# An up projection of the second layer's FFN as seven block products, with token halves of 320

## The chip, the cores and the metric

The kernel runs as one program on one NeuronCore of a Trainium2 chip. Its metric is the device time of one execution in microseconds, and the time given is the median of three executions. The engines are TensorE (PE, with its weight loads as a row of their own, PEld), VectorE (DVE), ScalarE (ACT), GpSimd (POOL) and SyncE (SP, which here only issues DMAs).

## The reference, cut to what matters

The reference is two layers of a transformer step over 640 tokens (128 prompt tokens and 512 latent tokens) of width 1024. A layer runs three token mixers, gates and an output projection; then comes the FFN, where the change lies.

```python
D_MODEL, D_FF = 1024, 2816
def _swiglu(h, w_in, w_out):
    a, b = jnp.split(h @ w_in, 2, axis=-1)      # w_in: 1024 x 5632
    return (jax.nn.silu(a) * b) @ w_out          # w_out: 2816 x 1024
def _layer(x, mod, lw, ...):
    sh1, sc1, g1, sh2, sc2, g2 = jnp.split(mod, 6, axis=-1)
    ...
    h = _rmsnorm(x, lw['norm2_g']) * (1.0 + sc2) + sh2
    x = x + g2 * _swiglu(h, lw['w_ffn_in'], lw['w_ffn_out'])
```

All inputs and outputs are float32.

## The kernel before

**Layout.** Activations lie transposed: 128 channels on the partitions, `KT` = 8 channel tiles, tokens along the free axis. The 640 tokens are cut in two halves, `HALF`: half 0 holds 256 tokens (128 prompt, 128 latent) and half 1 holds 384. Every operand of a large product is held as two float32r tiles, `hi` (a rounded copy, made on ACT by `split_hi`) and `lo` (the rest, made on DVE by `split_lo`, which subtracts `hi` from the value). Each product is three matmuls that accumulate in one PSUM bank: hi x hi, hi x lo, lo x hi (`mm3` and `mm_outer`).

**Weights.** `load_w` fetches a block of 128 x up to 1024 floats with one DMA on the SP queue into one of three `raw` buffers, and splits it into one of four `whi` and one of four `wlo` buffers. The buffers therefore set how far ahead weights can be fetched and split.

**FFN.** D_FF is cut in `FT` = 22 column tiles f of 128 columns. For each f and each half, `up_mm` computes a and b (2 outputs x 8 channel tiles x 3 matmuls = 48 matmuls), and `up_end` makes silu(a) * b (ACT, then DVE) and splits it into `ghi` and `glo`. The f are worked in parts, `FFN_PARTS` = 8, 8 and 6; after each part, `down` multiplies the part's g by the down weights for each of 8 output tiles n and both halves, and `x_add` adds the result to x. The first two f stand apart: their half 0 runs first, their half 1 behind it, so that `norm2(1)` (the normalisation of half 1) can run meanwhile. At the end of the last part and of the output projection, `tail` runs the last four n of one half first and then those of the other; before the last three units it calls `mid`, which starts the next normalisation on DVE and ACT.

**Order.** The program is written in one order, and a list scheduler places each instruction on its engine's queue when its operands and buffers are ready by its own reckoning, earliest in the program first; the queues then run in order. `plan` and `fill` deal out background work (in the first layer's FFN, the modulation rows `ada_rows` on DVE) at counted points.

Of the kernel before, what the change touches and what calls it, by code (L numbers as in the profile page):

```python
# [28 lines left out]
HALF = ((0, 256), (256, 384))  # L29
# [7 lines left out]
FFN_PARTS = ((0, 8), (8, 16), (16, 22))  # L37
# [10 lines left out]
class Kern:  # L48
    def __init__(self, ctx, nc, tc, io):
# [6 lines left out]
        self.hp = self.sb("hp", 1)  # L56
        self.w = self.sb("w", 4)
# [196 lines left out]
    def groups(self, h):  # L254
        return ((0, 0, 128), (1, 128, 256)) if h == 0 else ((1, 0, 384),)

    def square(self, h, k, x, pool):

        n = HALF[h][1]
        if k == 0:  # L260
            ss = self.ss[h] = pool.tile([P, 384], F32, tag="nss", name="nss", bufs=2)
            self.act.activation(ss[:, :n], x[:, k, :], AF.Square)
        else:
            ss = self.ss[h]
            sq = pool.tile([P, 384], F32, tag="nsq", name="nsq", bufs=2)
            self.act.activation(sq[:, :n], x[:, k, :], AF.Square)
            self.dve.tensor_tensor(ss[:, :n], ss[:, :n], sq[:, :n], op=ALU.add)
# [4 lines left out]
    def rstd(self, h, pool, ps, summed=False):  # L272
# [3 lines left out]
        r = pool.tile([P, 384], F32, tag="nr", name="nr", bufs=2)  # L276
# [4 lines left out]
    def h_tiles(self, h):  # L281
        n = HALF[h][1]
        return [self.hp.tile([P, KT, n], F32R, tag=f"h{h}{p}", name=f"h{h}{p}") for p in ("hi", "lo")]

    def modulate(self, l, which, h, k, xn, a, ht, pool):
# [4 lines left out]
        u = pool.tile([P, 384], F32, tag="nu", name="nu", bufs=2)  # L290
# [9 lines left out]
    def norm(self, l, which, h, x, a, pool, ps):  # L300
# [4 lines left out]
        for k in range(KT):  # L305
            t = pool.tile([P, 384], F32, tag="nt", name="nt", bufs=2)
            self.dve.tensor_tensor(t[:, :n], x[:, k, :], r[:, :n], op=ALU.mult)
            self.modulate(l, which, h, k, t[:, :n], a, ht, pool)
        return ht

    def start(self):
# [30 lines left out]
        for h in (0, 1):  # L342
            n = HALF[h][1]
            ps = self.Tp()
            for k in range(KT):
                sq = xp.tile([P, 384], F32, tag="nsq", name="nsq", bufs=2)
# [448 lines left out]
    def ret_values(self, l, act, pool):  # L795

        self.rproj = [self.dr.tile([P, NB, 256], F32, tag=f"rp{j}", name="rproj", bufs=1) for j in range(4)]
        for j in range(4):
            units = self.load_a(self.io["w_ret"][l, 2 + j], 2, 4, 256)
            for b in range(NB):  # L800
                ps = self.G()
                self.a_gemm(ps[:, :256], act, b, units)
                r = pool.tile([P, 384], F32, tag="gt", name="rvs", bufs=2)
# [200 lines left out]
    def gates(self, l, g, act, m, pool):  # L1004

        for n in range(KT):
            u = self.load_w(self.io["w_gate"][l, g, n], 1024)
            for h in (0, 1):
# [3 lines left out]
                t = pool.tile([P, 384], F32, tag="gt", name="gt", bufs=2)  # L1012
# [4 lines left out]
    def branch(self, l, g, act, yhi, ylo, m, pool, last):  # L1017
# [5 lines left out]
        def unit(n, h):  # L1023
# [4 lines left out]
            t = pool.tile([P, 384], F32, tag="gt", name="gt", bufs=2)  # L1028
# [26 lines left out]
    def m_split(self, m, h):  # L1055
        n = HALF[h][1]
        hi = self.hp.tile([P, KT, n], F32R, tag=f"h{h}hi", name=f"m{h}hi")
        lo = self.hp.tile([P, KT, n], F32R, tag=f"h{h}lo", name=f"m{h}lo")
# [20 lines left out]
    def out_proj(self, l, act, x, pool, mid):  # L1079
        wu = {}  # L1080

        def unit(n, h):
# [4 lines left out]
            self.square(h, n, x[h], pool)  # L1087
# [23 lines left out]
    def ffn(self, l, act, x, pool, xp, hook, a, b, mid):  # L1111
# [3 lines left out]

        def up_mm(fs, h, outs, hook=None):
            w = HALF[h][1]
            self.mm_outer([o[:, :w] for o in outs], [self.b_steps(*wu[f, j], 0, KT, act, h) for f in fs for j in range(2)], hook)

        def up_end(f, h, pa, pb):  # L1120
            o, w = HALF[h]
            s = pool.tile([P, 384], F32, tag="fs", name="fs", bufs=2)
            self.act.activation(s[:, :w], pa[:, :w], AF.Silu)
            self.dve.tensor_tensor(s[:, :w], s[:, :w], pb[:, :w], op=ALU.mult)
            self.split_hi(g[f][0][:, o:o + w], s[:, :w])
            self.split_lo(g[f][1][:, o:o + w], s[:, :w], g[f][0][:, o:o + w])
# [18 lines left out]
        for pi, (f0, f1) in enumerate(FFN_PARTS):  # L1145
            lastp = pi == len(FFN_PARTS) - 1
            for f in range(max(f0, 2), f1):
                load(f)
# [7 lines left out]
            if lastp:  # L1156
                self.log_exp_table()

            def down(n, h):
# [6 lines left out]
                if lastp:  # L1166
                    self.square(h, n, x[h], xp)
# [25 lines left out]
    def run(self):  # L1193
# [3 lines left out]
        for l in range(DEPTH):  # L1197
            if l > 0:
                xsrc = []
                for h in (0, 1):  # L1200
                    dt = self.dr.tile([P, KT, HALF[h][1]], F32, name=f"xs{h}")
                    self.pool.dma_start(out=dt, in_=x[h])
                    xsrc.append(dt)
                xctx.close()
# [31 lines left out]
            x = self.load_x(xp, xsrc)  # L1236
            mact = {}
# [13 lines left out]
            act2, nxt = {}, {}  # L1251

            def norm2(h, ps):
# [8 lines left out]
                act2[h] = self.norm(l, 1, h, x[h], norm2.a, xp, ps)  # L1262
            self.out_proj(l, mact, x, xp, lambda: norm2(0, self.Tp()))
            with ExitStack() as c3:
                fp = self.sb("ffn", 1, c3)
                if l == 0:
                    self.plan(34, (chain(self.ada_rows(0, 40, 48, adp), self.ada_rows(1, 0, 48, adp)), 56))

                    def norm1(h):
                        if h == 0:  # L1270
                            norm1.a = self.mod_scale(1, 0)
                        nxt[h] = self.norm(1, 0, h, x[h], norm1.a, xp, self.Tp())
                    self.ffn(l, act2, x, fp, xp, lambda ps: norm2(1, ps), 0, 1, lambda: norm1(0))
                else:
                    self.plan(34)
                    rf = []
# [136 lines left out]
```

## Time and profile before

| | |
|---|---|
| median of 3 executions (us) | 2488.35 (2484.45 to 2488.82) |
| time of the profiled execution (us) | 2487.65 |
| span of its profile, first to last instruction (us) | 2485.8 |
| mean granted TensorE clock | 0.996 |
| busy: PE, DVE, ACT, POOL (us) | 2419.1, 1511.3, 992.8, 177.0 |

The profile is of one execution. Busy time counts the instructions of an engine; matmuls are pipelined, so that their durations overlap and the distance from one start to the next is what a matmul costs. A line number is one of the code above, and can be that of a helper (L112 is `split_hi`, L115 `split_lo`, L120 the weight DMA).

### The profile page before, as it was taken

To read this page: it belongs to the slowest core of one execution; us is meant where nothing else is said; L and a number is where in the kernel's file an instruction comes from. 1 tells how busy PE (TensorE), PEld (TensorE's weight loads), DVE (VectorE), ACT (ScalarE), POOL (GpSimd) and SP (SyncE) were. 2 spreads that over 40 slices of the span, in tenths; PEclk is the share of its full clock that TensorE was granted. 3 is DMA by queue.
4 is the path that set the end of the run, shared out by engine and by line. 5 is a ranking of instruction groups with operands and counts; after the bars stand their busy time and mean duration, and the time that the engine had idled before them with its cause. 6 is when DMAs were issued, how large, how long until landed. Compare 5 with 4: busy or idle time off the path is not lost.

```text
span 2485.8 us, 42801 instructions
## 1 busy us (share of the span) xinstructions
PE 2419.1 (97%) x17236; PEld 2367.1 (95%) x17236; DVE 1511.3 (61%) x3463; ACT 992.8 (40%) x2102; POOL 177.0 (7%) x306
## 2 busy tenths in 40 slices
PE   8999999999999999999999999998999999999998
PEld 5999999999999999999999999998999999999997
DVE  5877686566787676485477867764663553333324
ACT  5656565422335221212375655653222352122123
POOL 0000210100010010010000012111000000000001
PEclk9999999999999999999999999999999999999999
DMA  6212322322553454463231123213232222222221
GB/s 263 75 60 63 105 78 65 96 91 70 196 175 111 153 178 153 128 193 102 66 126 55 60 75 114 69 61 126 62 109 69 77 68 85 78 69 76 69 75 62
DMA packets 70677, 248.94 MB, mean 100 GB/s; under 512 B 9840, under 2 KB 10064, under 8 KB 69584
## 3 DMA queue, kind: packets, MB, share of 16 engines
q1 hardware_dynamic: 46944, 164.12, 20.3%
q0 software_dynamic: 23248, 81.36, 10.1%
q8 instruction: 135, 2.21, 0.4%
q10 hardware_dynamic: 288, 0.73, 0.1%
q14 instruction: 62, 0.51, 0.1%
HBM read 225.97 MB, written 20.22 MB: 99 GB/s over the span
## 4 chain that ended last, share of the span: by engine, by line
PE 91%; DVE 4%; issue 2%; ACT 2%; DMA 1%; POOL 0%; DVEq 0%; ACTq 0%; POOLq 0%
PE G L131 13%; PE G L132 12%; PE G L133 12%; PE S L1107 8%; PE S L1106 8%; PE S L1105 8%; PE S L131 6%; PE S L132 6%; PE S L133 6%; PE O L855 1%; PE Tp L658 1%; PE S L825 1%; PE O L633 1%; PE O L632 1%; PE S L826 1%
## 5 line engine op out<-in xcount | busy, mean ns | idle before, releaser
L112 ACT CAST whi<-raw 128x1024 fp32r<-128x1024 f32 (+4 forms) x298 | 299.2, 1018 | 756.5 <-PE G L132 262.5
L115 DVE TENSOR_TENSOR wlo<-raw,whi 128x1024 fp32r<-128x1024 f32 (+4 forms) x298 | 349.2, 1182 | 370.7 <-ACT whi L112 368.6
L131 PE MATMUL G<-ghi,whi 128*128 128x256 f32 (+1 forms) x704 | 217.1, 309 | 3.1 <-DVE x L1067 3.1
L133 PE MATMUL G<-ghi,wlo 128*128 128x384 f32 (+1 forms) x704 | 216.4, 308 | 0.0
L132 PE MATMUL G<-glo,whi 128*128 128x384 f32 (+1 forms) x704 | 216.3, 308 | 0.0
L1105 PE MATMUL S<-h1hi,whi 128*128 128x384 f32 x640 | 214.0, 334 | 0.0
L1106 PE MATMUL S<-h1lo,whi 128*128 128x384 f32 x640 | 213.9, 334 | 0.0
L1107 PE MATMUL S<-h1hi,wlo 128*128 128x384 f32 x640 | 213.9, 334 | 0.0
L1107 PE MATMUL S<-h0hi,wlo 128*128 128x256 f32 x704 | 199.2, 283 | 1.1 <-DVE wlo L115 0.9
L1106 PE MATMUL S<-h0lo,whi 128*128 128x256 f32 x704 | 198.8, 283 | 0.0
L1105 PE MATMUL S<-h0hi,whi 128*128 128x256 f32 x704 | 198.1, 282 | 0.0
L238 DVE SCALAR_TENSOR_TENSOR junk<-rawr,csr 128x1024 bf16<-128x1024 f32 x160 | 195.0, 1219 | 1.3
L131 PE MATMUL G<-whi,h1hi 128*128 128x256 f32 x624 | 179.0, 287 | 1.5 <-DVE mx L449 0.6
L133 PE MATMUL G<-whi,h1lo 128*128 128x256 f32 x624 | 177.2, 284 | 0.0
L132 PE MATMUL G<-wlo,h1hi 128*128 128x256 f32 x624 | 177.2, 284 | 0.0
L1067 DVE SCALAR_TENSOR_TENSOR x<-G,mod,x 128x128 f32<-128x128 f32 (+1 forms) x192 | 77.4, 435 | 138.0 <-PE G L133 137.5
L448 DVE TENSOR_REDUCE mx<-S 128x1 f32<-128x640 f32 (+1 forms) x160 | 113.0, 714 | 49.4 <-PE S L826 28.5
L1107 PEld LDWEIGHTS S<-h0hi,wlo 128*128 128x128 f32 x704 | 134.6, 191 | 2.8 <-DVE wlo L115 2.6
L131 PEld LDWEIGHTS G<-ghi,whi 128*128 128x128 f32 x704 | 132.1, 188 | 4.6 <-DVE x L1067 3.4
L1106 PEld LDWEIGHTS S<-h0lo,whi 128*128 128x128 f32 x704 | 134.3, 191 | 0.3
L1105 PEld LDWEIGHTS S<-h0hi,whi 128*128 128x128 f32 x704 | 134.3, 191 | 0.0
L131 PE MATMUL G<-whi,h0hi 128*128 128x256 f32 x416 | 121.6, 293 | 12.0 <-DVE rvs L808 11.7
(431 smaller groups left out, 6901.8 us busy)
## 6 DMA issues: line engine op xcount, KB each, us to landing
raw<-w_ffn_in SPq DMA_DIRECT2D x88, 512.0 KB, 3.6
rawr<-w_adat POOLq DMA_DIRECT2D x80, 512.0 KB, 4.0
raw<-w_gate SPq DMA_DIRECT2D x48, 512.0 KB, 3.3
raw<-w_ffn_out SPq DMA_DIRECT2D x32, 512.0 KB, 3.7
raw<-w_diff SPq DMA_DIRECT2D x24, 512.0 KB, 3.5
raw<-w_branch SPq DMA_DIRECT2D x24, 512.0 KB, 3.6
raw<-w_ret SPq DMA_DIRECT2D x24, 512.0 KB, 3.5
raw<-w_ada SPq DMA_DIRECT2D x16, 512.0 KB, 9.7
```

The costliest lines, as they stand in the source:

```text
L112: (eng or self.act).copy(hi, src)
L115: (eng or self.dve).tensor_tensor(lo, src, hi.bitcast(F32), op=ALU.subtract)
L131: self.pe.matmul(out, lh, rh, start=i == 0, stop=False)
L132: self.pe.matmul(out, lh, rl, start=False, stop=False)
L133: self.pe.matmul(out, ll, rh, start=False, stop=i == n - 1)
L238: self.tc.keep_in_program_order(d.scalar_tensor_tensor(junk, raw, 1.0, self.csr[:, i, :], op0=ALU.mult, op1=ALU.mult, accum_out=mod[:, n, ...
L448: self.dve.tensor_reduce(mx, sv, axis=AX.XY if len(sv.shape) == 3 else AX.X, op=ALU.max)
L632: self.pe.matmul(o[:, :n], vv, hi, start=i == 0, stop=False)
L1067: self.dve.scalar_tensor_tensor(x[h][:, n, c0:c1], ps[:, c0:c1], g[:, n, gi:gi + 1], x[h][:, n, c0:c1], op0=ALU.mult, op1=ALU.add)
L1105: self.pe.matmul(o, lh, rh, start=k == 0, stop=False)
L1106: self.pe.matmul(o, lh, rl, start=False, stop=False)
L1107: self.pe.matmul(o, ll, rh, start=False, stop=k == nk - 1)
```

## The change

The second layer's FFN computes f = 2 to 21 by Strassen's scheme. The product is seen as a 2 x 2 block product: the weights by (a, b) and by upper and lower half of the 1024 channels, the activations by channel half and token half. Seven block products of 128 x 512 by 512 x 320 take the place of eight. For that:

- `HALF` becomes 320 and 320 in the whole kernel. The hi and lo of the activations become one pair of tiles of 640 tokens, `self.ht`. Output tensors y0, y1 and the inputs x0, x1 follow.
- `w_ffn_in` is stored on the host as blocks (a upper, b lower) and (b upper, a lower). The first layer, and f = 0 and 1 of the second, still run eight products, from these blocks (`up_steps`).
- `ffn_forms`, once: `norm` of the second layer leaves its float32 result in eight tiles `us`; from them DVE makes the sums and differences of activation blocks, and ACT and DVE split them. One of them replaces the upper channels of half 1 in `ht`.
- `ffn_weights`, for each f: two loads as before (`r`, `q`), a third load of `r`'s block into `t` (two buffers), and an accumulating DMA on the POOL queue that adds the first block of the second source, twice, to both halves of `t`. DVE makes two further sums in `q`. Splits: 1024 columns of `r`, 512 of `q`, 1024 of `t`, 1024 of the new `q`.
- `ffn_seven`, for each f: seven products of 12 matmuls of 320 columns, and the combination of the results on DVE and ACT in the tiles `v` and `u` (one buffer each).
- `FFN_PARTS` becomes 6, 6, 5 and 5 in both layers, and `ghi`, `glo` have 6 buffers instead of 10. The scratch of the norms moves into a pool of its own, which is closed before `ffn_forms` and opened again for the last part. `plan` of the first layer's FFN follows the new number of points.

```diff
-HALF = ((0, 256), (256, 384))
+HW = 320
+HALF = ((0, HW), (HW, HW))
...
-FFN_PARTS = ((0, 8), (8, 16), (16, 22))
+FFN_PARTS = ((0, 6), (6, 12), (12, 17), (17, 22))
+GB = 6
+NC = 2
...
+        self.ht = [self.hp.tile([P, KT, T], F32R, name=f"h{p}") for p in ("hi", "lo")]
...
-        return ((0, 0, 128), (1, 128, 256)) if h == 0 else ((1, 0, 384),)
+        return ((0, 0, 128), (1, 128, HW)) if h == 0 else ((1, 0, HW),)
...
+    def modulate(self, l, which, h, k, xn, a, ht, pool, u=None):
 
         n = HALF[h][1]
         sh = self.mod[l][:, 24 * which:24 * which + 8, :]
         hi, lo = ht
-        u = pool.tile([P, 384], F32, tag="nu", name="nu", bufs=2)
+        if u is None:
+            u = pool.tile([P, HW], F32, tag="nu", name="nu", bufs=2)
...
+        hi, lo = self.ht
+        return hi[:, k, 128 * b:128 * b + 128], lo[:, k, 128 * b:128 * b + 128]
...
+    def ffn_forms(self, pool, us):
+        d = self.dve
+        hh, hl = self.ht
+        fo, so = slice(0, HW), slice(HW, T)
+        x67 = [pool.tile([P, 4, T], F32R, name=f"x67{p}") for p in ("hi", "lo")]
+        x5 = [pool.tile([P, 4, HW], F32R, name=f"x5{p}") for p in ("hi", "lo")]
+        for k in range(4):
+            p, q = us[k], us[4 + k]
+            d.tensor_tensor(q[:, so], q[:, so], p[:, so], op=ALU.subtract)
+            d.tensor_tensor(p[:, so], p[:, fo], p[:, so], op=ALU.subtract)
+            d.scalar_tensor_tensor(p[:, fo], q[:, so], -1.0, p[:, fo], op0=ALU.mult, op1=ALU.subtract)
+            d.scalar_tensor_tensor(q[:, fo], p[:, fo], -1.0, q[:, fo], op0=ALU.mult, op1=ALU.subtract)
+            for hi, lo, src in ((x67[0][:, k, :], x67[1][:, k, :], p), (x5[0][:, k, :], x5[1][:, k, :], q[:, so]),
+                                (hh[:, k, so], hl[:, k, so], q[:, fo])):
+                self.split_hi(hi, src)
+                self.split_lo(lo, src, hi)
+        def part(ts, k0, o):
+            return [t[:, k0:k0 + 4, o] for t in ts]
+        return {1: part(self.ht, 0, fo), 2: part(self.ht, 4, fo), 3: part(self.ht, 0, so), 4: part(self.ht, 4, so),
+                5: x5, 6: part(x67, 0, fo), 7: part(x67, 0, so)}
...
+    def ffn_weights(self, pool, src):
+        d = self.dve
+        raw = []
+        for i in range(2):
+            t = self.w.tile([P, 1024], F32, tag="raw", name="raw", bufs=3)
+            self.nc.sync.dma_start(out=t, in_=src[i])
+            raw.append(t)
+        r, q = raw
+        fo, so = slice(0, 512), slice(512, 1024)
+        def split(x, n, own, hi_tag, lo_tag):
+            kw = {} if own is self.w else {"bufs": 2}
+            hi = own.tile([P, n], F32R, tag=hi_tag, name=hi_tag, **kw)
+            lo = own.tile([P, n], F32R, tag=lo_tag, name=lo_tag, **kw)
+            self.split_hi(hi, x)
+            self.split_lo(lo, x, hi)
+            return hi, lo
+        b13 = split(r, 1024, self.w, "whi", "wlo")
+        t = pool.tile([P, 1024], F32, tag="ts", name="ts", bufs=2)
+        self.nc.sync.dma_start(out=t, in_=src[0])
+        self.nc.gpsimd.dma_start(out=t.rearrange("p (a n) -> p a n", a=2), in_=src[1][:, fo].unsqueeze(1).to_broadcast([P, 2, 512]), accum_op=ALU.add)
+        t57 = split(t, 1024, pool, "thi", "tlo")
+        b2 = split(q[:, so], 512, self.w, "whi", "wlo")
+        d.tensor_tensor(q[:, fo], t[:, fo], r[:, so], op=ALU.add)
+        d.tensor_tensor(q[:, so], q[:, fo], q[:, so], op=ALU.add)
+        t64 = split(q, 1024, pool, "thi", "tlo")
+        def part(u, c0):
+            return [x[:, c0:c0 + 512] for x in u]
+        return {1: part(b13, 0), 2: b2, 3: part(b13, 512), 4: part(t64, 512), 5: part(t57, 0), 6: part(t64, 0), 7: part(t57, 512)}
...
+    def ffn_seven(self, pool, W, X, single, pair, ghi, glo):
+        d, a = self.dve, self.act
+        fo, so = slice(0, HW), slice(HW, T)
+        s1, s7 = (t[:, :HW] for t in single)
+        p26, p45 = pair[0][:, :, :HW], pair[1][:, :, :HW]
+        def prod(i, o):
+            (wh, wl), (xh, xl) = W[i], X[i]
+            for k in range(4):
+                c = slice(128 * k, 128 * k + 128)
+                self.pe.matmul(o, wh[:, c], xh[:, k, :], start=k == 0, stop=False)
+                self.pe.matmul(o, wh[:, c], xl[:, k, :], start=False, stop=False)
+                self.pe.matmul(o, wl[:, c], xh[:, k, :], start=False, stop=k == 3)
+        v = pool.tile([P, 4, HW], F32, tag="v", name="v", bufs=1)
+        u = pool.tile([P, HW], F32, tag="u", name="u", bufs=1)
+        ga, gb = (v[:, i:i + 2, :].rearrange("p a n -> p (a n)") for i in (0, 2))
+        def twice(x):
+            return x.unsqueeze(1).to_broadcast([P, 2, HW])
+        prod(1, s1)
+        a.copy(u, s1)
+        prod(2, p26[:, 0])
+        prod(6, p26[:, 1])
+        d.tensor_tensor(v[:, 0:4:2, :], p26, twice(u), op=ALU.add)
+        a.activation(v[:, 0, :], v[:, 0, :], AF.Silu)
+        prod(7, s7)
+        d.tensor_tensor(u, v[:, 2, :], s7, op=ALU.add)
+        prod(5, p45[:, 1])
+        d.tensor_tensor(v[:, 2, :], v[:, 2, :], p45[:, 1], op=ALU.add)
+        prod(4, p45[:, 0])
+        d.tensor_tensor(v[:, 1:4:2, :], p45, twice(u), op=ALU.add)
+        a.activation(v[:, 1, :], v[:, 1, :], AF.Silu)
+        prod(3, s1)
+        d.tensor_tensor(v[:, 2, :], v[:, 2, :], s1, op=ALU.add)
+        d.scalar_tensor_tensor(ga, gb, -1.0, ga, op0=ALU.mult, op1=ALU.mult)
+        self.split_hi(ghi, ga)
+        self.split_lo(glo, ga, ghi)
...
+        def up_steps(f, j, h):
+            (ph, pl), (qh, ql) = wu[f] if j == 0 else wu[f][::-1]
+            return self.b_steps(ph, pl, 0, 4, act, h) + self.b_steps(qh, ql, 512, 4, act, h, 4)
         def up_mm(fs, h, outs, hook=None):
-            w = HALF[h][1]
-            self.mm_outer([o[:, :w] for o in outs], [self.b_steps(*wu[f, j], 0, KT, act, h) for f in fs for j in range(2)], hook)
+            self.mm_outer([o[:, :HW] for o in outs], [up_steps(f, j, h) for f in fs for j in range(2)], hook)
...
+        def hold(f):
+            g[f] = (pool.tile([P, T], F32R, tag="ghi", name="ghi", bufs=GB), pool.tile([P, T], F32R, tag="glo", name="glo", bufs=GB))
 
         def load(f):
-            for j in range(2):
-                wu[f, j] = self.load_w(io["w_ffn_in"][l, f, j], 1024)
-            g[f] = (pool.tile([P, T], F32R, tag="ghi", name="ghi", bufs=10), pool.tile([P, T], F32R, tag="glo", name="glo", bufs=10))
+            wu[f] = [self.load_w(io["w_ffn_in"][l, f, j], 1024) for j in range(2)]
+            hold(f)
...
+                if us is not None and f >= NC:
+                    if f == NC:
+                        self.sctx.close()
+                        xfctx = ExitStack()
+                        X = self.ffn_forms(self.sb("xf", 1, xfctx, "right"), us)
+                    W = self.ffn_weights(pool, io["w_ffn_in"][l, f])
+                    hold(f)
+                    single = [self.Tp() for _ in range(2)] if f % 2 else [self.G() for _ in range(2)]
+                    self.ffn_seven(pool, W, X, single, [self.S() for _ in range(2)], *g[f])
+                    continue
...
+                if us is not None:
+                    xfctx.close()
+                    self.open_scratch()
...
+            us = None
+            if l == 1:
+                us = [fp.tile([P, T], F32, tag="glo" if k % 2 else "ghi", name="us", bufs=GB) for k in range(KT)]
...
+                self.plan(44, (self.ada_rows(0, 40, 48, adp), 8, 0.0, 0.08), (self.ada_rows(1, 0, 48, adp), 48, 0.08, 0.95))
...
+                self.plan(0)
...
+def blocks(a, b):
+    return np.stack([np.concatenate([a[:, :, :512], b[:, :, 512:]], axis=2), np.concatenate([b[:, :, :512], a[:, :, 512:]], axis=2)], axis=1)
...
-OUTS = {"y0": (128, KT, 256), "y1": (128, KT, 384), "nret": (DEPTH, 128, 512), "ndk": (DEPTH, 128, 512),
+OUTS = {"y0": (128, KT, HW), "y1": (128, KT, HW), "nret": (DEPTH, 128, 512), "ndk": (DEPTH, 128, 512),
```

## Rows read from the trace of the kernel before

**Rows 1.** Page, busy time of each engine, its share and instructions.

```profile
PE 2419.1 (97%) x17236; PEld 2367.1 (95%) x17236; DVE 1511.3 (61%) x3463; ACT 992.8 (40%) x2102; POOL 177.0 (7%) x306
```

**Rows 2.** Page, the chain that ended last, by engine.

```profile
PE 91%; DVE 4%; issue 2%; ACT 2%; DMA 1%; POOL 0%; DVEq 0%; ACTq 0%; POOLq 0%
```

**Rows 3.** Windows, second FFN: us; busy us (instructions) of each; clock, DMA.

```profile
core 0: us, PE busy (x) PEld busy (x) DVE busy (x) ACT busy (x) POOL busy (x), PEclk, DMA share, GB/s
2210.05:2224.12 14.07, 14.07 (x98) 14.07 (x97) 4.23 (x6) 3.69 (x6) 0.00 (x0) 1.00 0.24 77
...
2123.00:2165.00 42.00, 42.00 (x292) 42.00 (x291) 16.16 (x27) 6.83 (x7) 0.00 (x0) 1.00 0.28 88
```

**Rows 4.** Timeline of PE, one f: start us, duration us, instruction.

```profile
2204.30 0.28 PE L1105 MATMUL S<-h0hi,whi 128*128 128x256 f32 x1
...
2210.05 0.34 PE L1105 MATMUL S<-h1hi,whi 128*128 128x384 f32 x1
...
2218.37 0.28 PE L1105 MATMUL S<-h0hi,whi 128*128 128x256 f32 x1
```

**Rows 5.** Timeline of PE, matmuls of 320 columns, first and last of seven.

```profile
340.59 0.31 PE L826 MATMUL S<-K2z,Q 128*128 128x320 f32 x1
...
341.47 0.31 PE L826 MATMUL S<-K2z,Q 128*128 128x320 f32 x1
```

**Rows 6.** Groups by form, DVE and ACT: count, busy us, mean ns, idle before.

```profile
L115 DVE TENSOR_TENSOR wlo<-raw,whi 128x1024 fp32r<-128x1024 f32 x260 | 315.0, 1222 | 338.2 <-ACT whi L112 336.8 <-PE G L133 0.2
...
L115 DVE TENSOR_TENSOR ptl<-Tp,pth 128x512 fp32r<-128x512 f32 x64 | 43.0, 685 | 8.1 <-ACT pth L112 7.5
...
L839 DVE SCALAR_TENSOR_TENSOR dp<-dp,dz 128x640 f32<-128x640 f32 x32 | 28.2, 882 | 0.6
...
L1124 DVE TENSOR_TENSOR fs<-fs,S 128x384 f32<-128x384 f32 x40 | 21.9, 548 | 0.0
...
L1124 DVE TENSOR_TENSOR fs<-fs,S 128x256 f32<-128x256 f32 x44 | 18.4, 419 | 50.7 <-ACT fs L1123 50.7
...
L112 ACT CAST whi<-raw 128x1024 fp32r<-128x1024 f32 x260 | 269.3, 1050 | 710.4 <-PE G L132 244.3 <-PE S L1106 218.9 <-PE S L132 171.8
...
L112 ACT CAST ghi<-fs 128x384 fp32r<-128x384 f32 x44 | 22.6, 513 | 80.4 <-DVE fs L1124 80.4
```

**Rows 7.** Windows (columns as in rows 3) before and at f = 2, second layer.

```profile
2028.00:2034.00 6.00, 6.00 (x37) 6.00 (x36) 0.06 (x1) 0.74 (x1) 0.00 (x0) 1.00 0.00 0
2034.00:2038.00 4.00, 3.47 (x22) 2.82 (x21) 3.66 (x4) 3.37 (x6) 0.00 (x0) 1.00 0.28 77
```

**Rows 8.** Timeline of DVE: two splits of 1024 columns in one piece.

```profile
2050.52 2.36 DVE L115 TENSOR_TENSOR wlo<-raw,whi 128x1024 fp32r<-128x1024 f32 x2 [6.12 <-ACT whi L112]
```

**Rows 9.** Windows (columns as in rows 3) around PE's idle of 498 to 502 us.

```profile
493.00:496.00 3.00, 3.00 (x28) 3.00 (x27) 0.85 (x4) 0.63 (x1) 1.06 (x2) 1.00 1.01 350
499.00:501.00 2.00, 0.00 (x0) 0.00 (x0) 1.18 (x1) 0.00 (x0) 0.00 (x0) 1.00 0.68 182
503.00:504.00 1.00, 1.00 (x7) 1.00 (x6) 0.00 (x0) 0.00 (x0) 0.31 (x1) 0.50 0.77 299
505.00:506.00 1.00, 1.00 (x8) 1.00 (x8) 0.00 (x0) 0.00 (x0) 0.00 (x0) 0.69 0.02 8
```

**Rows 10.** Timeline of PE, first products of the second layer.

```profile
1258.41 0.45 PE L1107 MATMUL S<-whi,h0lo 128*128 128x416 f32 x1 [1.02 <-DVE h0lo L115]
```

**Rows 11.** Timeline of PE, end of a part: up and down matmuls interleave.

```profile
2165.07 0.28 PE L1106 MATMUL S<-h0lo,whi 128*128 128x256 f32 x1
2165.19 0.34 PE L131 MATMUL G<-ghi,whi 128*128 128x384 f32 x1
```

**Rows 12.** DMA issues: queue, count, KB each, median us to landing.

```profile
raw<-w_ffn_in SPq DMA_DIRECT2D x88, 512.0 KB, 3.6
rawr<-w_adat POOLq DMA_DIRECT2D x80, 512.0 KB, 4.0
...
x<-x POOLq DMA_DIRECT2D x1, 1536.0 KB, 12.8
...
x<-xs POOLq DMA_DIRECT2D x1, 1536.0 KB, 8.0
```

More of the change, by code (lines that the diff above doesn't have):

```diff
@@ L260, in square @@
         if k == 0:
[L261 removed]
+            ss = self.ss[h] = pool.tile([P, HW], F32, tag="nss", name="nss", bufs=2)
             self.act.activation(ss[:, :n], x[:, k, :], AF.Square)
@@ L264, in square @@
             ss = self.ss[h]
-            sq = pool.tile([P, 384], F32, tag="nsq", name="nsq", bufs=2)
+            sq = pool.tile([P, HW], F32, tag="nsq", name="nsq", bufs=2)
             self.act.activation(sq[:, :n], x[:, k, :], AF.Square)
@@ L281, in h_tiles @@
     def h_tiles(self, h):
-        n = HALF[h][1]
-        return [self.hp.tile([P, KT, n], F32R, tag=f"h{h}{p}", name=f"h{h}{p}") for p in ("hi", "lo")]
-    def modulate(self, l, which, h, k, xn, a, ht, pool):
+        o, n = HALF[h]
+        return [t[:, :, o:o + n] for t in self.ht]
+    def modulate(self, l, which, h, k, xn, a, ht, pool, u=None):
         n = HALF[h][1]
@@ L298, in modulate, with norm @@
         self.split_lo(lo[:, k, :], u[:, :n], hi[:, k, :])
-    def norm(self, l, which, h, x, a, pool, ps):
+    def norm(self, l, which, h, x, a, pool, ps, us=None):
         n = HALF[h][1]
@@ L305, in norm @@
         for k in range(KT):
-            t = pool.tile([P, 384], F32, tag="nt", name="nt", bufs=2)
+            t = pool.tile([P, HW], F32, tag="nt", name="nt", bufs=2)
             self.dve.tensor_tensor(t[:, :n], x[:, k, :], r[:, :n], op=ALU.mult)
-            self.modulate(l, which, h, k, t[:, :n], a, ht, pool)
+            self.modulate(l, which, h, k, t[:, :n], a, ht, pool, us and us[k][:, HW * h:HW * h + n])
         return ht
@@ L345, in start @@
             for k in range(KT):
-                sq = xp.tile([P, 384], F32, tag="nsq", name="nsq", bufs=2)
+                sq = xp.tile([P, HW], F32, tag="nsq", name="nsq", bufs=2)
                 self.act.activation(sq[:, :n], x[h][:, k, :], AF.Square)
@@ L802, in ret_values @@
                 self.a_gemm(ps[:, :256], act, b, units)
-                r = pool.tile([P, 384], F32, tag="gt", name="rvs", bufs=2)
+                r = pool.tile([P, HW], F32, tag="gt", name="rvs", bufs=2)
                 if j < 2:
@@ L1077, in tail, with out_proj @@
             unit(n, b)
-    def out_proj(self, l, act, x, pool, mid):
+    def out_proj(self, l, act, x, mid):
         wu = {}
@@ L1112, in ffn @@
+    def ffn(self, l, act, x, pool, hook, a, b, mid, us=None):
         io = self.io
@@ L1261, in norm2, with norm1 @@
                     self.log_exp_table()
[L1262 to L1276, printed above, removed]
-                    self.ffn(l, act2, x, fp, xp, lambda ps: norm2(1, ps), 1, 0, lambda: rf.append(self.rstd(1, xp, self.Tp())))
-                    self.final(1, x[1], rf[0])
-                    self.final(0, x[0], self.rstd(0, xp, self.Tp()))
+                act2[h] = self.norm(l, 1, h, x[h], norm2.a, self.scr, ps, us)
+            self.out_proj(l, mact, x, lambda: norm2(0, self.Tp()))
+            if l == 0:
+                self.plan(44, (self.ada_rows(0, 40, 48, adp), 8, 0.0, 0.08), (self.ada_rows(1, 0, 48, adp), 48, 0.08, 0.95))
+                def norm1(h):
+                    if h == 0:
+                        norm1.a = self.mod_scale(1, 0)
+                    nxt[h] = self.norm(1, 0, h, x[h], norm1.a, self.scr, self.Tp())
+                self.ffn(l, act2, x, fp, lambda ps: norm2(1, ps), 0, 1, lambda: norm1(0))
+            else:
+                self.plan(0)
+                rf = []
+                self.ffn(l, act2, x, fp, lambda ps: norm2(1, ps), 1, 0, lambda: rf.append(self.rstd(1, self.scr, self.Tp())), us)
+                self.final(1, x[1], rf[0])
+                self.final(0, x[0], self.rstd(0, self.scr, self.Tp()))
+            fctx.close()
             if l == 0:
```

42 lines of the change are left out of this document (23 added, 19 removed).

## The prediction, made before the change was run

> **What bounds the kernel now.** I read the page's busy times first: PE is busy for nearly the whole span, DVE for three fifths, ACT for two fifths [rows 1]. Busy PE can hide waits, so the chain that ended last came next: nine tenths of it are PE [rows 2]. Then the stage of the change alone. The reader is to see there that PE and its weight loads fill a window of one f to the last hundredth, that the window is 14.07 us, and that DVE needs only 4.23 us of it [rows 3]. So in the second layer's FFN columns streamed through PE are time, one for one, and DVE has about 10 us of idle in each f that it may spend. The question is whether the change's new DVE work fits, and where it doesn't.
>
> **PE's saving.** One f is 96 matmuls now. In the timeline 48 of 256 columns take 2210.05 - 2204.30 = 5.75 us, 119.8 ns each, and 48 of 384 columns 8.32 us, 173.3 ns each [rows 4]; the mean is 146.6 ns. Six steps between matmuls of 320 columns take 0.88 us, 146.7 ns each [rows 5]. So halves of 320 cost PE what 256 and 384 cost together, in every stage, and the gain is in the count: 84 matmuls instead of 96 for each of 20 f. 20 x 12 x 146.6 ns = **-35.2 us**. An f becomes 84 x 146.6 = 12.31 us.
>
> **DVE and ACT inside an f.** For subtractions and products the rows give 419 ns at 256 columns, 548 at 384, 685 at 512 and 1222 at 1024, and 882 for a three-operand one of 640 [rows 6]. Along that line 320 columns are 0.49 us and 640 are 0.82. The weights take three splits of 1024 and three instructions of 512: 3 x 1.22 + 3 x 0.69 = 5.73 us. The combination takes three of 640 (two of them read PSUM, one splits g), the product of 0.88, and three of 320: 3 x 0.82 + 0.88 + 3 x 0.49 = 4.81 us. Together 10.5 us of 12.31, 86%. ACT has casts of 1024 at 1.05 three times, 0.59 or so for 512, and five operations of 320 to 640 at 0.43 to 0.75: under 6 us [rows 6]. Both fit by sum. By order: the splits `thi`, `tlo` of the next f are the tight place. The pair for products 6 and 4 is freed when product 4 ends, sixth of seven, and is needed when the next f starts its third product, three products of 1.76 us later: 5.3 us. In them DVE owes 0.82 (sum after product 4), 1.22 for the split of products 5 and 7 if that is late, and the 1.22 of the split itself behind ACT's 1.05: about 3 us when the queue keeps that order. 2 us are to spare. I charge 0.2 us an f for hand-overs that fall badly, **+4** in all; below, nothing; above, DVE paces the f (a rival).
>
> **The start of f = 2.** Now DVE is idle from 2028 to 2034 (0.06 us busy in 6), while PE finishes f = 0 and 1, and in the four us behind it PE loses about one, waiting for the split of weights whose buffers have only just come free [rows 7]. The forms go into this gap and are larger than it. For each of four channel tiles: four sums of 320, splits of 640, 320 and 320: 6 x 0.49 + 0.82 = 3.75 us, 15.0 in all. Behind them in program order stand the ends of f = 0 and 1 (about 2 us) and the weights of f = 2 (5.7). That is 22.7 us; some 1.5 fit into gaps of `norm2(1)`, and instructions in a row overlap by 0.08 us (two splits take 2.36, not 2.44 [rows 8]), some 3.0 over 38 of them. 18.2 us from 2028 end at 2046.2. PE has only products 1 and 2 that need no form or sum, 3.5 us from about 2035: it is out of work at 2038.4 and waits 7.8 us, of which one was there before. Such a wait can drop the clock: after four us without a matmul it stood at 0.50 for some 3 us (503 to 506) [rows 9], half of which is lost; 6.8 and some of that, I take **+7.5**. Below: 3, if the queue lets the weights' sums ahead and product 6 follows the forms tile by tile; above: 13.5, without overlap and with the clock.
>
> **Layer boundary and other tails.** `mid` starts the next half's normalisation behind the last three units. At the first layer's end these are 3 x 18 matmuls of 173.3 ns = 9.4 us and become 3 x 15 of 146.6 = 6.6: 2.8 us less cover. Half 0 grows by 64 columns, about 0.17 us on DVE for each channel tile (two instructions at 0.07, the rest on the group of 192), 1.3 in all. PE already waits 1.02 us there on DVE [rows 10], so nothing hides the rest: up to 4.1, I take **+3**; below, 0. The output projection's tail shortens by 3 x 24 x 26.7 ns = 1.9 us and has the same longer norm, twice; DVE has room there, I take **+0.5** (0 to 5). The last norm has more columns behind the last matmul but fewer before; 0.
>
> **Ends of parts.** In the second layer, g of the last f of a part is ready only after a sum of 0.49, the product 0.88, ACT's cast of 640 (0.75) and the split 0.82: 3 us behind the last matmul. The first down unit has the other four or five f to start on, 12 or 15 x 146.6 ns = 1.8 to 2.2 us, and the scheduler may interleave a second one, as it mixes up and down matmuls now [rows 11]. **+2** for four ends (0 to 5). A fourth part adds 16 x_adds in each layer; PE and DVE in a down stage show 42.00 of 42 and 16.16 of 42 [rows 3], so they cost nothing; without that idle DVE each would cost its 0.5 to 0.7 us. Modulation rows move only in count per f: nothing. The h tiles shared by both halves are written one channel tile and half at a time, so I see no new wait.
>
> **The third load and the accumulating DMA.** Each f adds 512 KB on SP and 512 KB of adding on POOL. A plain load lands after 3.6 us on SP and 4.0 on POOL [rows 12]. No row shows an accumulate: below, it is the plain 4.0; above, the worst POOL transfers, three times the bytes, took 8.0 and 12.8 [rows 12]. I take a value near the row with the same queue and bytes, 5. With two `t` buffers a sum is wanted about 20 us after its load can start, so 3.6 + 5 is hidden and I charge 0. Bandwidth: 2 MB (2.5 with a second read of the target) in 12.3 us is 170 to 210 GB/s, and windows reach 350 [rows 9].
>
> **Sum.** -35.2 + 4 + 7.5 + 3 + 0.5 + 2 = -18.2. From the span, 2485.8 - 18.2 = 2467.6; around it lie 2487.65 - 2485.8 = 1.85, so 2469.5. The profiled execution lies 0.7 below the median of the three and inside their spread. I say **2470 us**; with all terms low or high together it would be 2455 or 2484, and its own range is 2457 to 2482.
>
> **Rivals.**
> *The loads form a loop (slower).* Three raw buffers serve two loads an f. The second load of an f takes the buffer that DVE's first sum of the f before must have read, and that sum needs the accumulated `t`. If the plain load of `t` stands behind that second load on SP's queue, a loop closes: two loads, 3.6 and 1.5 more (512 KB at 350 GB/s [rows 9]), the accumulate, the sum 0.69, hand-overs 0.3: 6.1 us and the accumulate. Above 6.2 us for the accumulate the loop paces the f. At 8.0 it is 14.1, 1.8 too long for 16 f (the first of each part is fetched during a down stage): +29, 2499 us. At 12.8: +105, 2575. The gain is gone from 7.3 us on. For it: SP mostly waits for buffers. Against: the buffer of `t` itself is free much earlier, and a scheduler that goes by readiness puts it ahead. Chance 0.17.
> The Trainium skill, "Collectives: The Full Stack", section "The bandwidth ceiling: the fold count and why AG ≠ RS ≠ AR", speaks for this rival: an add in the DMA path reads two sources for each chunk, so that a reduce moves at half the rate of a copy. No run here shows it; an accumulate of 8.0, twice the plain row, would be an estimate by that page, with the rival's 2499 us.
>
> *DVE paces the f.* 10.5 us leave 1.8 for 14 instructions, many behind ACT, PE or a DMA. With 0.18 us more on each, an f takes 13.0: 0.7 x 16 = 11 more, 2481 us; with 0.25 more, 14.0 and 2497. For it: in order, one late operand holds all behind it. Against: long splits can be done an f ahead. Chance 0.16.
>
> *The forms are hidden too.* The scheduler mixes forms with products and the boundary loses nothing: 2485.8 - 35.2 + 3 + 3 + 1.85 = 2458 us. For it: it already interleaves halves and parts [rows 11]. Against: the DVE sum above. Chance 0.13.
>
> **How the numbers follow.** The forecast has 0.54. A change of 0.2%, 5 us, is about what can be told from none. Faster (under 2483.4): the forecast but 0.03, the last rival, and 0.08 of DVE's, 0.72. Same: 0.03, 0.05 of DVE's and 0.02 of the loop's, 0.10. Slower: 0.15 and 0.03, 0.18. The range 2455 to 2496 leaves out most of the loop and a little at either end.
>
> **What would show it.** Right: products of 320 columns 147 ns apart, an f of 12.3 us, DVE busy 85% in it; one idle stretch of PE of 6 to 9 us at f = 2, ended by DVE; some 3 us at the layer boundary. Wrong: an f longer than 12.6 us with PE waiting for `tlo` or `thi` (then see what DVE waited for: a DMA is the loop, nothing is DVE's own pace); an accumulate that lands after more than 6 us; or PE waits in stages that only the halves touch.

## The result, and the profile after

The changed kernel takes 2519.64 us (median of 4; 2517.14 to 2527.19), the kernel before 2487.95 (median of 4): a ratio of 1.0135, 95% interval 1.0111 to 1.0159. It is 32 us slower where 18 us less was forecast, and lies outside the range. The profiled execution took 2517.14 us.

The page of the changed kernel, beside [rows 1, 2]: PE's own work fell by little, and the chain has more DVE and DMA in it.

```profile
PE 2410.0 (96%) x16996; PEld 2347.0 (93%) x16996; DVE 1661.3 (66%) x3695; ACT 1037.7 (41%) x2170; POOL 200.8 (8%) x326
...
PE 83%; DVE 8%; DMA 3%; ACT 3%; issue 3%; POOL 0%; DVEq 0%; POOLq 0%; ACTq 0%; SPq 0%
```

Windows of the changed kernel in the second layer's FFN: from behind the end of the first part to the end of the second, the seven products in it (with few down units at its end), and the end of the first part (after the span: busy time and count of PE, PEld, DVE, ACT, POOL, then the granted clock, DMA share and GB/s):

```profile
2124.00:2240.00 116.00, 110.73 (x738) 109.41 (x736) 70.61 (x100) 37.35 (x52) 7.14 (x6) 0.99 0.50 133
2165.00:2237.00 72.00, 67.70 (x446) 66.65 (x444) 47.79 (x62) 27.75 (x40) 5.95 (x5) 0.98 0.55 143
2100.00:2124.00 24.00, 18.68 (x113) 17.54 (x113) 13.39 (x20) 6.14 (x10) 0.00 (x0) 0.93 0.20 59
```

PE, full to the last hundredth before [rows 3], now has holes, the most at the end of a part. DVE is busy 47.79 of the 72 us of the products, 66%, where the forecast had 85% of a shorter f: its load is not the bound. (The first window, at 61%, also holds the first part's down units, where DVE has less to do.) The largest waits of PE in this stage, 2050 to 2502 (total, times, longest):

```profile
PE G L135 <- ACT ghi L116: 10.4, 4, 3.0
PE S L1182 <- DVE v L1196: 9.2, 6, 2.8
PE S L1182 <- DVE v L1201: 4.7, 4, 1.5
PE S L1182 <- DVE v L1203: 3.2, 4, 0.9
PE G L135 <- DVE x L1070: 1.9, 4, 0.6
```

Most of it is a product (L1182 to L1184) that may not write its PSUM pair `S` because DVE has yet to read it, or the first down unit that waits for g of a part's last f. None is for `thi` or `tlo`, the place that the prediction called tight. DVE's side, in the groups of its instructions by line for the same stretch, shows what it stood at:

```profile
L1203 DVE TENSOR_TENSOR v<-S,u 128x640 f32<-128x640 f32 x20 | 16.5, 824 | 25.7 <-PE S L1184 25.7
L1163 DVE TENSOR_TENSOR raw<-ts,raw 128x512 f32<-128x512 f32 x19 | 13.1, 691 | 52.2 <-DMA raw<-w_ffn_in 31.4 <-DMA ts<-w_ffn_in 20.7
```

L1163 is the first weight sum: DVE stands at it for 52 us, waiting for the second load or for the accumulate. L1203 is the sum that follows product 4; it waits 25.7 us for PE while PE waits for DVE. How DVE's wait reaches PE inside a part, at f = 8, DVE and then PE:

```profile
2190.60 0.69 DVE L1163 TENSOR_TENSOR raw<-ts,raw 128x512 f32<-128x512 f32 x1 [4.99 <-DMA ts<-w_ffn_in]
2191.21 0.82 DVE L119 TENSOR_TENSOR glo<-v,ghi 128x640 fp32r<-128x640 f32 x1
2192.13 0.82 DVE L1196 TENSOR_TENSOR v<-S,u 128x640 f32<-128x640 f32 x1
```

```profile
2193.01 0.53 PE L1182 MATMUL S<-hhi,whi 128*128 128x320 f32 x1 [2.23 <-DVE v L1196]
...
2198.16 0.31 PE L1182 MATMUL S<-hhi,thi 128*128 128x320 f32 x1
```

L1196 reads products 2 and 6 of f = 8 and stands in the queue behind the weight sum of f = 10, which waits 4.99 us for its accumulate. The matmul at 2193.01 is the first of product 2 of f = 9 and needs the pair that L1196 frees. Product 4 of f = 8 comes only behind it, at 2198.16. The last us of the first part, PE and then DVE:

```profile
2105.55 0.45 PE L135 MATMUL G<-ghi,whi 128*128 128x320 f32 x2
...
2108.12 0.42 PE L1182 MATMUL S<-hhi,thi 128*128 128x320 f32 x1 [1.53 <-DVE v L1201]
...
2113.19 0.57 PE L135 MATMUL G<-ghi,whi 128*128 128x320 f32 x2 [3.03 <-ACT ghi L116]
```

```profile
2105.45 0.82 DVE L1196 TENSOR_TENSOR v<-S,u 128x640 f32<-128x640 f32 x1 [0.87 <-PE S L1184]
2106.31 0.49 DVE L1199 TENSOR_TENSOR u<-v,Tp 128x320 f32<-128x320 f32 x1
2106.72 0.95 DVE L119 TENSOR_TENSOR wlo<-raw,whi 128x768 fp32r<-128x768 f32 x1
2107.58 0.48 DVE L1201 TENSOR_TENSOR v<-v,S 128x320 f32<-128x320 f32 x1
2108.10 0.49 DVE L1206 TENSOR_TENSOR v<-v,Tp 128x320 f32<-128x320 f32 x1
2110.19 0.82 DVE L1203 TENSOR_TENSOR v<-S,u 128x640 f32<-128x640 f32 x1 [1.61 <-PE S L1184]
2111.55 0.82 DVE L1207 SCALAR_TENSOR_TENSOR v<-v 128x640 f32<-128x640 f32 x1 [0.54 <-ACT v L1204]
```

The matmul at 2108.12 is the first of product 4. It starts at the moment when L1201 is done. L1201 adds *product 5*, from the other half of the pair; nothing that product 4 computes with comes from it. Product 4 therefore runs last, behind everything that stands ahead of L1201 in DVE's queue, and behind it comes the whole chain of sum, silu, product and cast, 3.03 us with PE idle.

Outside the seven products the changed kernel had already lost time: the first FFN starts at 791.8 us against 784.7, the second layer's f = 2 at 2050.2 against 2034.8.

### The profile page after: what moved, and what is told of

The parts are those of the page before. It is cut to its first block, busy times and chain, and to the rows that moved or that the text cites. A ratio compares the mean times of both kernels' runs of the same rounds, so it can differ in the third digit from the quotient of the medians.

```text
span 2515.4 us, 42864 instructions
## 1 busy us (share of the span) xinstructions
PE 2410.0 (96%) x16996; PEld 2347.0 (93%) x16996; DVE 1661.3 (66%) x3695; ACT 1037.7 (41%) x2170; POOL 200.8 (8%) x326
## 4 chain that ended last, share of the span: by engine, by line
PE 83%; DVE 8%; DMA 3%; ACT 3%; issue 3%; POOL 0%; DVEq 0%; POOLq 0%; ACTq 0%; SPq 0%
PE G L135 12%; PE G L136 11%; PE G L137 11%; PE S L135 6%; PE S L136 6%; PE S L137 6%; PE S L1110 4%; PE S L1109 4%; PE S L1108 4%; DMA ts<-w_ffn_in 2%; PE O L860 1%; PE S L1182 1%; PE S L1183 1%; PE S L1184 1%; PE Tp L663 1%
## 5 line engine op out<-in xcount | busy, mean ns | idle before, releaser
L135 PE MATMUL G<-whi,hhi 128*128 128x256 f32 x1040 | 301.2, 290 | 12.5 <-DVE rvs L813 9.9
L137 PE MATMUL G<-whi,hlo 128*128 128x256 f32 x1040 | 297.0, 286 | 0.0
L136 PE MATMUL G<-wlo,hhi 128*128 128x256 f32 x1040 | 296.3, 285 | 0.0
L135 PE MATMUL G<-ghi,whi 128*128 128x320 f32 x704 | 219.5, 314 | 17.2 <-ACT ghi L116 10.4
L136 PE MATMUL G<-glo,whi 128*128 128x320 f32 x704 | 220.1, 313 | 1.2 <-DVE glo L119 1.2
L137 PE MATMUL G<-ghi,wlo 128*128 128x320 f32 x704 | 219.5, 312 | 0.0
L1110 PE MATMUL S<-hhi,wlo 128*128 128x320 f32 x704 | 217.1, 310 | 1.3 <-DVE wlo L119 1.3
L1109 PE MATMUL S<-hlo,whi 128*128 128x320 f32 x704 | 217.8, 310 | 0.2 <-DVE hlo L119 0.2
L1108 PE MATMUL S<-hhi,whi 128*128 128x320 f32 x704 | 216.8, 309 | 0.0
L136 PEld LDWEIGHTS G<-wlo,hhi 128*128 128x128 f32 x1040 | 200.3, 193 | 0.1
L135 PE MATMUL S<-hhi,whi 128*128 128x320 f32 x512 | 160.6, 314 | 2.8 <-DVE gt L1037 2.7
L137 PE MATMUL S<-hhi,wlo 128*128 128x320 f32 x512 | 158.4, 309 | 0.0
L136 PE MATMUL S<-hlo,whi 128*128 128x320 f32 x512 | 158.3, 309 | 0.0
```

Of the source, the lines that this page charges most:

```text
L135: self.pe.matmul(out, lh, rh, start=i == 0, stop=False)
L136: self.pe.matmul(out, lh, rl, start=False, stop=False)
L137: self.pe.matmul(out, ll, rh, start=False, stop=i == n - 1)
L1108: self.pe.matmul(o, lh, rh, start=k == 0, stop=False)
L1109: self.pe.matmul(o, lh, rl, start=False, stop=False)
L1110: self.pe.matmul(o, ll, rh, start=False, stop=k == nk - 1)
```

## The experiments

Theories: A, the weight sum waits in DVE's in-order queue for late loads; B, ends of parts; C, halves and parts in the whole kernel; D, DVE's load; later F and G, the order inside the PSUM pair. E and H are rivals that the expectations name. Each time is the median of 4 runs, timed beside the kernel before (2486.5 to 2488.3 in the three sets; so some 2 us between runs of different sets tell nothing).

**Eight products again, the rest of the change left.**

```diff
-            if l == 1:
+            if False:
                 us = [fp.tile([P, T], ...) for k in range(KT)]
```

> The changed kernel, but with the eight products in the second layer's FFN too (no sums, no third load): halves of 320, four parts and six g buffers stay. Theory A (the weight sums stand in VectorE's in-order queue and wait for late loads and accumulates; the loss is in the seven-product stage): the shift of +15 us at the start of f = 2 and one more part end in that FFN, some 4 to 6 us, stay, so 2505 to 2511 us, and the seven products themselves cost 8 to 15 us. Rival C (what came in with the halves and the parts is the whole loss, the seven products gain their 35 us less their own waits): 2535 us or more. Rival D (VectorE's new work alone is the loss): 2488 us, as before.

2508.55 us, ratio 1.0085 (1.0068 to 1.0102). 21.8 us of the loss have nothing to do with Strassen; the seven products cost 11.1 more. A's range holds; C's and D's don't. The seven products do not gain their 35 us, but two thirds of the loss came in with the halves and parts.

**The halves alone** (beside the edit above, which keeps the eight products).

```diff
-FFN_PARTS = ((0, 6), (6, 12), (12, 17), (17, 22))
-GB = 6
+FFN_PARTS = ((0, 8), (8, 16), (16, 22))
+GB = 10
...
-self.plan(44, (self.ada_rows(0, 40, 48, adp), 8, 0.0, 0.08), (self.ada_rows(1, 0, 48, adp), 48, 0.08, 0.95))
+self.plan(34, (chain(self.ada_rows(0, 40, 48, adp), self.ada_rows(1, 0, 48, adp)), 56))
```

> As the last one, but with the three parts of 8, 8 and 6, ten g buffers and the old plan of modulation rows: of the change only the halves of 320 and the shared tiles are left. If parts cost by their ends (one more in each layer, 4 to 6 us each), this is 8 to 12 us below the kernel with four parts: 2495 to 2499. If the halves cost nothing, as the prediction had it for PE, 2488. If the halves carry all of the shift, 2503 to 2508, as with four parts.

2499.18 us, ratio 1.0049 (1.0034 to 1.0064): halves of 320 cost 12.5 us, four parts 9.4. In its trace the first FFN starts 8.6 us late and the first layer ends 11.4 late; the second layer adds 1. No one wait holds it: from 298 to 785 us PE's steps of over 330 ns, each less the 147 of one matmul, add up to 22.2 us against 17.7 before, which is 4.5 of the 8.6.

**No accumulate.** The accumulating DMA (L1160) is taken out, so that four of the seven products lack one term of their weights.

> The changed kernel without the accumulating DMA: the third load stays, nothing is added to it, so products 5, 7, 6 and 4 get weights that lack one term. Theory A: VectorE's 20.7 us of waiting for ts fall away; part of it was PE's, some 8 to 15 us, so 2505 to 2512 us. Rival B (the ends of parts and the clock behind them make the loss): unchanged, 2517 to 2520. Rival D: unchanged, 2517 to 2520.

2505.49 us, 14.1 less than the changed kernel: A is right about the accumulate. But the four waits for `ghi` at the ends of parts stayed at 10.4 us, and it is only 3.1 below eight products.

**t by DVE.**

```diff
-        self.nc.sync.dma_start(out=t, in_=src[0])
-        self.nc.gpsimd.dma_start(out=t..., in_=src[1][:, fo]..., accum_op=ALU.add)
+        for c in (fo, so):
+            d.tensor_tensor(t[:, c], r[:, c], q[:, fo], op=ALU.add)
```

> The changed kernel with the sums of t made by VectorE (two of 512 columns from the two loaded tiles) instead of the third load and the accumulate. VectorE gets 20 x 2 x 0.69 = 28 us more. Theory A: the wait for ts is gone, but the sums still wait for the second load in the same queue: 2505 to 2518. Rival D (VectorE's load is the bound): up to 28 us slower, 2535 to 2547.

2512.46 us, 7.2 less, with 28 us more work on DVE: D falls. The accumulate is gone here too; beside the run that only leaves it out, the additional work costs 7.0.

**The two weight sums on GpSimd** (L1163, L1164: `d.tensor_tensor` becomes `self.pool.tensor_tensor`).

> The changed kernel with the two sums that make the weights of products 6 and 4 (512 columns each) moved from VectorE to GpSimd. The accumulate and all loads stay; only the place where the wait stands is another queue. Theory A (what is lost inside a part is lost because the sum waits in VectorE's queue, ahead of the sums that free PSUM): the waits for DMA leave VectorE, 8 to 14 us of the 14.1 that leaving out the accumulate gave come back, 2505 to 2512. Rival E (the weights themselves are late, whichever engine waits for them): no gain, 2516 to 2525, with PE waiting for thi or tlo.

2509.94 us, 9.7 less, though the sums themselves take 1.35 and 1.68 us there instead of 0.69. Moving the wait out of DVE's queue helped; rival E's sign, PE waiting for `thi`, came as well, with 4.1 us.

**t by GpSimd** (the same two sums as with DVE, on `self.pool`).

> The changed kernel with the sums of t made by GpSimd from the two loaded tiles (two of 512 columns) instead of the third load and the accumulating DMA. GpSimd took 1.09 us for a product of 320 columns, so about 3.5 us an f by that row. VectorE has nothing more to do. Theory A: as without the accumulate, 2503 to 2510; the sum then waits for the second load and 3.5 us. Rival E: if lateness of t itself counts, the same as with t on VectorE, 2510 to 2515.

2519.53 us, no gain: a miss. The two sums took 1.66 us each, and DVE waits for them at the same place in its queue, 15.3 us in 14 times. PE's waits for `ghi` stay at 10.4 us.

**Two lines exchanged.**

```diff
-        d.tensor_tensor(v[:, 2, :], v[:, 2, :], p45[:, 1], op=ALU.add)
         prod(4, p45[:, 0])
+        d.tensor_tensor(v[:, 2, :], v[:, 2, :], p45[:, 1], op=ALU.add)
```

> The changed kernel with two lines exchanged: product 4 is written ahead of VectorE's addition of product 5. Both halves of a PSUM pair are one tile, and in the trace product 4 waits for that addition (1.5 us at three of four ends of parts, 2.8 at 2431). Theory F (this ordering inside the pair costs in every f and at the ends): 6 to 15 us faster than the changed kernel, 2505 to 2513. If PE has other matmuls to do in these places: within 3 us of it, 2517 to 2522.

2472.89 us, ratio 0.9948 (0.9931 to 0.9964): **46.8 us less than the changed kernel**, three times the most that was expected of theory F, and 35.7 less than eight products with the same halves and parts. All of PE's waits of 0.6 us or more in 2050 to 2460 of its trace, and then the window that answers to the first one above:

```profile
PE Tp L279 <- DVE nss L271: 3.0, 1, 3.0
PE G L135 <- DVE x L1070: 2.3, 4, 0.6
PE S L1182 <- DVE v L1196: 1.0, 1, 1.0
```

```profile
2113.00:2220.00 107.00, 107.00 (x732) 107.00 (x731) 70.95 (x102) 38.63 (x54) 7.14 (x6) 1.00 0.55 141
```

Product 4 now follows product 5 at once, 2096.68, and product 3 at 2098.44 closes the last f of the part. All 36 matmuls of the first two down units, 30 of which the changed kernel had spent earlier as filling, are now left, starting from 2100.20 to 2105.33, and cover the chain to g; one wait of 0.57 us remains at the end of that part:

```profile
2096.53 0.31 PE L1184 MATMUL S<-x5hi,tlo 128*128 128x320 f32 x1
2096.68 0.31 PE L1182 MATMUL S<-hhi,thi 128*128 128x320 f32 x1
...
2098.44 0.31 PE L1182 MATMUL Tp<-hhi,whi 128*128 128x320 f32 x1
...
2100.20 0.31 PE L135 MATMUL G<-ghi,whi 128*128 128x320 f32 x1
...
2106.21 0.38 PE L135 MATMUL G<-ghi,whi 128*128 128x320 f32 x1 [0.57 <-DVE x L1070]
```

And DVE still stands at the weight sum, nearly as long as in the changed kernel:

```profile
L1163 DVE TENSOR_TENSOR raw<-ts,raw 128x512 f32<-128x512 f32 x19 | 13.1, 692 | 44.2 <-DMA raw<-w_ffn_in 22.2 <-DMA ts<-w_ffn_in 21.9
```

Nor did DVE's load change. In four f of the second part PE is full beside a DVE that is busy 76%:

```profile
2150.00:2198.00 48.00, 48.00 (x330) 48.00 (x329) 36.51 (x50) 21.91 (x32) 3.57 (x3) 1.00 0.63 158
```

**Five parts in the second layer.** `((0, 5), (5, 10), (10, 14), (14, 18), (18, 22))`, without the exchange.

> The changed kernel with five parts in the second layer's FFN (5, 5, 4, 4, 4) instead of four; the first layer as it is. One end of a part more, and 16 more additions to x. Rival B (each end costs what the profile shows around it, 6 to 8 us with the clock behind it): 2525 to 2529. If an end costs what it costs with eight products (9.4 us for two, 4.7): 2524. The prediction's own price, half a microsecond for each end: 2520.

2517.75 us, 1.9 less. One end more costs nothing that can be told: B's 6 to 8 us for each fall. The end is not free by itself: in the trace PE's waits for `ghi` grow from 10.4 us in 4 to 13.4 in 5, while those for L1196 and L1203 fall by 4.6 in all.

**The read of the pair taken out, the lines in their order.**

```diff
-        d.tensor_tensor(v[:, 2, :], v[:, 2, :], p45[:, 1], op=ALU.add)
+        d.tensor_tensor(v[:, 2, :], v[:, 2, :], u, op=ALU.add)
         prod(4, p45[:, 0])
```

> The changed kernel, its lines in their order, but the addition between products 5 and 4 takes u instead of product 5 from PSUM, so that one term of the result is wrong and nothing reads the pair of products 4 and 5 before both are written. VectorE has as many instructions as before. Theory G (product 4 waits because the pair is one tile, of which the other half is being read): like the kernel with the two lines exchanged, 2468 to 2478. Rival H (the exchange only gave the scheduler a luckier order): 2505 to 2520, as changed.

2473.23 us, the same as with the exchange. It is the read of one half of the tile that held back the writing of the other: G, and not rival H, a luckier order by the exchange alone. How much of the price is waiting at the tie and how much the order that the scheduler makes because of it, the two runs don't separate.

**The exchange, and no accumulate.**

> The two lines exchanged, and the accumulating DMA left out as well (products 5, 7, 6 and 4 get weights that lack one term). In the changed kernel leaving it out gave 14.1 us. Theory G (the late sum cost time only because PE's product 4 was tied to VectorE's queue): now it gives nothing, 2470 to 2475. Rival A (the late sum costs by itself): 8 to 14 us less, 2459 to 2465.

2472.72 us, 0.2 less. What was worth 14.1 us in the changed kernel is worth nothing once product 4 is free.

**The exchange, and the first layer's parts as before** (8, 8, 6, ten g buffers, the old plan; the second layer keeps four parts).

> The two lines exchanged, and the first layer's FFN back at three parts of 8, 8 and 6 with ten g buffers and the old plan of modulation rows. With eight products four parts cost 9.4 us over three in both layers together, so 4.7 by half: 2467 to 2470. If it was the second layer's end that cost, or the plan and not the end (a fifth part there cost nothing): 2471 to 2475.

2470.46 us, 2.4 less, half of the 4.7 reckoned, and between the two ranges.

**As the last one, and the first layer's halves as before.** The halves are set for each layer, and x passes between the layers through one DRAM tile.

```diff
-HALF = ((0, HW), (HW, HW))
+HALF = ((0, 256), (256, 384))
+HALF2 = ((0, HW), (HW, HW))
...
+                HALF1, HALF = HALF, HALF2
+                act = {h: self.h_tiles(h) for h in (0, 1)}
...
+                dt = self.dr.tile([P, KT, T], F32, name="xs")
+                for h, (o, n) in enumerate(HALF1):
+                    self.pool.dma_start(out=dt[:, :, o:o + n], in_=x[h])
+                xsrc = [dt[:, :, o:o + n] for o, n in HALF]
```

> As the last one, and the first layer's token halves back at 256 and 384; the second layer has 320 and 320. The halves alone cost 12.5 us, of which 11.4 had gathered by the end of the first layer: 2455 to 2460, well under both kernels. If the second layer loses what the first regains (its stages are the same, but lost 1 us there), 2465 to 2470.

2460.39 us, ratio 0.9890 (0.9874 to 0.9907): 10.1 less, 0.4 above the range expected, and under both kernels by 28 and 59 us. Sizes of halves in one layer make that difference (with x passed through one tile); the h tiles shared by both halves are still there and cost nothing that shows.

## Why the prediction was wrong

**The step that failed** is "by order", in the part on DVE and ACT inside an f: it took the splits `thi`, `tlo` for the tight place and asked of DVE's queue only what the weights need. It didn't follow each product to what its PSUM tile waits for. `p45` is one tile of two banks. Program order has product 5, then L1201 that reads it, then product 4 into the same tile, so product 4 waits for L1201 although they touch different banks. In the program of every f that ties PE to DVE's in-order queue. Its price is shown from both sides, by the exchange (46.8 us) and by taking the read out (46.4).

**How the price builds up.** PE's steps of over 200 ns in the stage, each less 147, hold 50.1 us in the changed kernel (2050 to 2502) and 5.9 in the exchanged one (2049 to 2455): 44 of the 46.8 us are idle and slow steps of PE there. DVE's queue stands at the weight sum L1163 for 52.2 and 44.2 us. With the tie, product 4 comes late on PE's queue (at f = 8 behind product 2 of f = 9), and PE stands at pairs whose reads L1163 holds up. So removing the accumulate gives 14.1 us with the tie and 0.2 without. A waiting in-order queue was harmless until another engine waited in the middle of it. The other part is at the ends: product 4 last, most of the down units already used up, 3 us of idle three times and 1.3 once, and a granted clock of 0.93 by the mean of the window around the first of them (11 matmuls there of 200 to 330 ns; 102 in the stage, 11.8 us over their 147). A split of the 46.8 into these parts was not measured.

**Term by term.**
- *PE's saving, -35.2*: right. With the tie gone, seven products take 35.7 us less than eight under the same halves and parts, net of the 2 us of the next item, and products run 147 ns apart.
- *Hand-overs, +4, and the start of f = 2, +7.5*: both too high. In the second FFN of the exchanged kernel PE's steps over 200 ns hold 6.0 us too much, with eight products 4.0: 2 us for both terms. The forms run while PE is full from 2035 to 2050; the scheduler mixed them with other work, as the rival "the forms are hidden too" had it.
- *Layer boundary, +3*: right; the halves alone add 2.8 there (8.6 to 11.4 us).
- *Halves elsewhere, 0*: wrong by 9.7 (12.5 with the boundary). The reckoning by columns holds, 147 ns for 320; what grew are PE's short waits (4.5 of the 8.6 us ahead of the first FFN are its long steps). Which of them matter, and why halves of 320 make them longer, stays open.
- *Ends of parts, +2, and a fourth part, nothing*: four parts cost 9.4 us with eight products. With the exchange the first layer's share is 2.4, and a fifth part in the second layer cost nothing. In the traces of the two kernels with eight products, 7.8 us apart, 2.4 are there at the end of the first layer too, 3.7 by the second layer's FFN, 5.5 in its last down units; the rest comes in the last 20 us. What makes it stays open.
- *The third load and the accumulating DMA, 0*: its size was near (5 taken, 5.8 median from issue to landing, 5.1 to 9.1 in the trace, 6 of 20 above the 6 us named as a sign), the "20 us" were not there: `t` stays taken until its own split, which waits for `thi`. For f = 10 the load starts at 2179.6 and the sum waits for the accumulate until 2190.6. Its cost of 0 holds only without the tie.

```profile
ts<-w_ffn_in SPq DMA_DIRECT2D x20, 512.0 KB, 3.6
ts<-w_ffn_in POOLq DMA_DIRECT2D x20, 512.0 KB, 5.8
```

The terms give 12.5 + 9.4 + 46.8 - 35.7 = 33.0, and the changed kernel stands 32.9 above the 2486.7 us timed beside the first two. That confirms nothing: each term is a difference between two of the same runs, so that they must add up.

That the exchanged kernel's 2472.9 lies near the 2470 forecast confirms the saving, not the sum, and is in part luck: halves and parts cost 21.8 instead of 5.5, 2 us came where 11.5 were charged, and the two errors go opposite ways.

**The rivals.** The loop of loads named the right wait (DVE at the sum, ended by a DMA) but not how it reaches PE: nothing is left of it in the exchanged kernel, with the same loads. DVE's pace is out: the sum of 10.5 us for an f was right (the instructions' means in the changed kernel's trace give 10.5 again), and in the exchanged kernel PE is full beside the same work. The sign named beforehand, "PE waits in stages that only the halves touch", came true, with the kernel of eight products and halves of 320.

The Trainium skill, "Collectives: The Full Stack", section "The bandwidth ceiling: the fold count and why AG ≠ RS ≠ AR", states for rings of three ranks and more that a reduce, with two sources to read, moves at half a copy's rate. Carried over to this DMA, an estimate of twice a plain load's time; here it took 5.8 us against 3.6 for the plain load of the same tile on SP and 3.9 to 4.0 for loads of this size on POOL, some 1.5 to 1.6 times. By the exchanged kernel without it that time is not what cost.

The Trainium skill, "PSUM — Partial Sum Buffer", section "PSUM bank collisions raise a hardware error", asks that PSUM be guarded by bank and quadrant. The pair, one tile of two banks, was guarded as a whole, which is more than that rule asks; the exchange and the run without the read show what that cost here.

## What to carry to other kernels

When several results share one PSUM tile, follow the program order of its writes and reads: here a read of one part between two writes made the second write wait, though it went to another bank. Write all producers first, or give each its own tile. An in-order queue that waits is free only as long as no other engine needs something from behind the wait; so reckon a late transfer not by its landing but by what is queued after the instruction that waits for it, and undo a tie before speeding up what seems late. And a change of tile sizes needs a run of its own: equal columns for the busiest engine do not mean equal waits.

## What the runs showed of the hardware that was not expected

GpSimd took 1.35 to 1.68 us for a sum of 512 columns where VectorE took 0.69. An accumulating DMA of 512 KB into SBUF landed after 5.8 us by the median and 9.1 at the worst, and its issue kept GpSimd busy for 1.19 us, against 0.53 for a plain load there.
